# SBUF placement of matmul operands, by their distance modulo 256 bytes, in a hybrid decoder block

## Chip, cores and metric

One Trainium2 chip, one of its cores. The time is device microseconds of one execution of the program; where several executions are shown, the median counts.

## What is computed

One block of a hybrid decoder on `x` of 1 x 256 x 1024 (float32): a normed input feeds three token mixers (retention, a gated short convolution, sparse attention), their outputs are merged by gates, and a gated feed-forward follows.

```python
h = rms_norm(x, attn_norm_w)
z = h @ w_in
y_ret, y_sc, y_nsa = retention(...), sb * causal_dwconv(sc * sx), nsa_attention(...)
merged = g_ret * (y_ret @ w_ret_out) + g_sc * (y_sc @ w_sc_out) + g_nsa * (y_nsa @ w_nsa_out)
x = x + merged @ w_mix_out
u = causal_dwconv(rms_norm(x, ffn_norm_w) @ w_ffn_up)
a, v = split(u); x = x + (silu(a) * v) @ w_ffn_down
return rms_norm(x, final_norm_w)
```

## The kernel before, in words

All weights come from memory as float32 in pieces of 128 x 2048. A piece is an `Item`: `load` brings it in two halves of 128 x 1024 into the ring `raw` (line 123), `split` makes of each half a high part `whi` (ScalarE, line 131) and a remainder `wlo` (VectorE, line 132), both of the type float32r, in a ring of five pairs (line 114, later three more, line 957, and for a while one pair `w_m`, line 319). A product is three matmuls, high by high, high by low, low by high (`mm3`, line 158). `stream` (line 170) walks a list of items, loading two ahead and splitting one ahead; its order and that of `items` set the order of all work, and TensorE takes its instructions in that order.

There are two ways to multiply by a piece. `f_consume` (line 188) makes an output with features on the partitions: the weights are the operand that is loaded into the array (128 columns at a time), the activations `hT`, `xw`, `x2w` or `h2` stream past, 256 columns (all tokens); a piece is 48 matmuls of 256 columns. The pieces kc, vc, ks, kw, nq, scx, sb, rq, rk and up are of this kind. `t_pair` (line 205) and `dn_consume` (line 1078) make an output with tokens on the partitions: 128 tokens of the activations are loaded, and 512 columns of the weights stream. The pieces mg, rv, rg, o_sc, o_nsa, o_ret, mix and dn are of this kind.

**Where the operands lie.** A tile takes its bytes per partition behind the one before it in its pool, pool after pool, in steps of 32 bytes; what counts here is the place modulo 256 bytes, and the distance of a matmul is the place of its loaded operand less that of its streamed one. `whi` and `wlo` (4,096 bytes), `hTh`, `hTl` (8,192), `rstd` and `ones` (1,024 and 512) are multiples of 256, so `whi`, `wlo` and `hT` are at distance 0 of each other. Then comes `x_s` (line 238) of `HD + 2048` columns; with `HD = 32` that is 8,320 bytes, 128 more than a multiple of 256. So `ynsah`, `ynsal` (line 241; `x2w`, line 962, takes their place later) and `yscl` (line 242) lie 128 bytes off, while `ysch`, which takes the place of `x_s`, doesn't. `mT` (line 958) takes the places of `ysch` and `yscl`: one at 0, one at 128. The 64 bytes of `line`, with `warm` and `rs0` of 32 each, bring what follows back to 0: `w_m`, the six `thg` buffers (line 718), `yreth`, `yretl`, `act` and the second ring. `h2` (line 1039) takes the place of `hT`.

The attention scores (`soft_step`, line 529) load `qs` and stream the keys `kdh`, `kdl`, at 128 x 272 and, for the second 128 tokens, 128 x 256 columns. A row of keys is 528 columns for each of four groups, 2,112 bytes or 64 modulo 256, so the distance goes with the group: 160, 96, 32 and 224 bytes for groups 0 to 3 with 272 columns (`qs` lies 160 bytes behind `kd`), and 64 less for those of 256 columns, whose keys start 272 columns (1,088 bytes) on.

| operands of line 156 | columns streamed | matmuls | distance before |
|---|---|---|---|
| `hT`, `h2` by `whi`, `wlo` | 256 | 1,920 | 0 |
| `x2w` by `whi`, `wlo` | 256 | 192 | 128 |
| `xw` (`ynsah`, `ynsal`) by `whi`, `wlo`, `w_m`, kc and vc | 256 | 96 | 128 |
| weights by `hT`, `yret`, `act` (mg, rv, rg, o_ret, dn) | 512 | 840 | 0 |
| weights by `ynsah`, `ynsal` (o_nsa) | 512 | 96 | 128 |
| weights by `ysch` / `yscl` (o_sc) | 512 | 64 / 32 | 0 / 128 |
| weights by `mT` (mix) | 512 | 64 / 32 | 0 / 128 |

Of the kernel before, what the change touches and what calls it, by code (L numbers as in the profile page):

```python
# [11 lines left out]
F32 = mybir.dt.float32  # L12
F32R = mybir.dt.float32r
# [5 lines left out]
S = 256  # L19
D = 1024  # L20
KB = 8
# [15 lines left out]
CM_Z, CM_T, CM_C0, CM_C1, CM_ANY, CM_BLK, CM_SEL = 0, 128, 384, 400, 416, 418, 422  # L37
CM_N = 486

HD = 32  # L40


def _schedule():
# [20 lines left out]
def kernel(  # L64
# [24 lines left out]
    wpool = ctx.enter_context(pool("wpool"))  # L89
# [15 lines left out]
    RAWB, SPB = 4, 5  # L105
    WARM = 8

    def ring(p, nb):
        def get():
            return [p.tile([128, 1024], F32R, tag=n, name=n, bufs=nb) for n in ("whi", "wlo")]  # L110

        return [get] * nb

    splitters, count = ring(wpool, SPB), [0]

    class Item:
        def __init__(self, srcs, consume, pull=0):
            self.srcs, self.consume, self.pull = srcs, consume, pull
            self.raw, self.parts = [], []

        def load(self):
# [4 lines left out]

        def split(self):
            for (ap, n), r in zip(self.srcs, self.raw):
                hi, lo = splitters[count[0] % len(splitters)]()
                count[0] += 1  # L130
                A.copy(hi[:, :n], r[:, :n])  # L131
                V.tensor_sub(lo[:, :n], r[:, :n], f32(hi[:, :n]))  # L132
                self.parts.append((hi, lo))
# [5 lines left out]
    def then(it, f, before=False):  # L139
        old = it.consume  # L140

        def go(parts):
            if before:
                f()
            old(parts)
            if not before:
                f()

        it.consume = go
        return it  # L150

    def piece(name, i, consume, **kw):
        return Item(halves(name, i), consume, **kw)
# [34 lines left out]
    def f_consume(act, evac, kmajor=False):  # L188


        def go(parts):
            ah, al = act() if callable(act) else act
            ps = bank("mm")
            order = [(b, k) for k in range(KB) for b in range(2)] if kmajor else [(b, k) for b in range(2) for k in range(KB)]
            for n, (b, k) in enumerate(order):
                hi, lo = parts[b]
                c = slice(k * 128, (k + 1) * 128)
                o = ps[:, b * 256 : (b + 1) * 256]
                start = n == 0 if kmajor else k == 0
                mm3(o, (hi[:, c], lo[:, c]), (ah[:, k, :], al[:, k, :]), start, k == KB - 1)  # L200
            evac(ps)

        return go
# [25 lines left out]


    yp = mix_es.enter_context(pool("yp"))
    hT = [yp.tile([128, KB, S], F32R, tag=n, name=n) for n in ("hTh", "hTl")]
    M = []
    rstd = yp.tile([128, S], F32, name="rstd")
    ones = yp.tile([128, 128], F32, name="ones")
# [7 lines left out]
    nc.scalar.dma_start(x_s[:, 0 : HD + S], xh)  # L243
    V.memset(ones, 1.0)
    V.memset(mhalf, -0.5)
    yp.tile([128, 16], F32, name="line")
    warm = yp.tile([128, 2], F32, name="warm")
    A.activation(warm, mhalf, AF.Exp)
    pw = bank("aux")
# [47 lines left out]
    def head_h(half):  # L297
        for k in range(4 * half, 4 * half + 4):
            V.scalar_tensor_tensor(xT_s[:, k, :], xT_s[:, k, :], attw(k), rstd, op0=OP.mult, op1=OP.mult)  # L299
            if k % 2 == 1:  # L300
                c = slice(k - 1, k + 1)
                A.copy(hT[0][:, c, :], xT_s[:, c, :])
                V.tensor_sub(hT[1][:, c, :], xT_s[:, c, :], f32(hT[0][:, c, :]))  # L303
# [12 lines left out]
    cp_es = ExitStack()  # L316
    cp = cp_es.enter_context(pool("cp"))

    splitters += [lambda: (lambda z: (z[:, 0, :], z[:, 1, :]))(yp.tile([128, 2, 1024], F32R, tag="m", name="w_m"))]
    blk = {}  # L320

    def cmp_raw_evac(kv):
        def evac(ps):
            p4 = ps.rearrange("p (b t) -> p b t", b=2)
            d = cp.tile([128, 4, S], F32, tag="dd", name="dd", bufs=2)
            dv = d.rearrange("p (b two) t -> p b two t", two=2)
            for par in range(2):
                r = slice(par * 64, par * 64 + 64)
                V.tensor_tensor(dv[0:64, :, par, :], p4[r], rstd[r].unsqueeze(1).to_broadcast([64, 2, S]), op=OP.mult)  # L329
            nc.scalar.dma_start(d[64:128, :, 0 : S - 1], d[0:64, :, 1:S])  # L330
            later(lambda: cmp_blocks(kv, d))

        return evac
# [16 lines left out]
    def key_evac(name):  # L350
        def evac(ps):
            p4 = ps.rearrange("p (b t) -> p b t", b=2)
            for par in range(2):
                r = slice(par * 64, par * 64 + 64)
                o = slice(64 - par * 64, 128 - par * 64)
                kv4 = [k.rearrange("p (b two) t -> p b two t", two=2) for k in kd]
                for t in range(2):
                    c = KCOL[(name, t)]
                    src = p4[r, :, t * 128 : (t + 1) * 128]
                    dst = [k[r, :, par, c : c + 128] for k in kv4]  # L360
                    A.copy(dst[0], src)
                    V.tensor_sub(dst[1], src, f32(dst[0]))  # L362
                c = min(KCOL[(name, t)] for t in range(2))
                for k in kv4:
                    nc.gpsimd.dma_start(k[o, :, par, c : c + 256], k[r, :, par, c : c + 256])

        return evac
# [148 lines left out]
    def q_evac(g):  # L516
        def evac(ps):
            p4 = ps.rearrange("p (b t) -> p b t", b=2)
            qs = at.tile([128, 2, 2, S], F32R, tag="qs", name="qs", bufs=2)
            for par in range(2):  # L520
                r = slice(par * 64, par * 64 + 64)
                o = slice((1 - par) * 64, (1 - par) * 64 + 64)
                A.mul(qs[r, par], p4[r], 0.125)
                V.scalar_tensor_tensor(qs[o, par], p4[r], 0.125, f32(qs[r, par]), op0=OP.mult, op1=OP.subtract)
            qs_t[g] = qs

        return evac
# [149 lines left out]
    def scx_evac(j):  # L677
        def evac(ps):
            sx = sc_tmp.tile([128, S], F32, tag="sx", name="sx", bufs=1)
            A.copy(sx, ps[:, S : 2 * S])  # L680
            V.tensor_mul(sx, ps[:, 0:S], sx)
            u = sc_tmp.tile([128, S], F32, tag="u", name="u", bufs=4)
            conv3(sx, [cvt[:, CV_SC + 8 * i + j : CV_SC + 8 * i + j + 1] for i in range(3)], u)
            sc_prod[j] = u

        return evac

    def sb_evac(i):
        def evac(ps):
            for b in range(2):  # L690
                j = 2 * i + b
                u = sc_prod[j]
                V.tensor_mul(u, ps[:, b * S : (b + 1) * S], u)
                A.copy(ysc[0][:, j, :], u)
                V.tensor_sub(ysc[1][:, j, :], u, f32(ysc[0][:, j, :]))

        return evac
# [1 line left out]
    rsh = at.tile([128, 2], F32, name="rsh")  # L699

    def scx(j, **kw):
        return piece("scx", j, f_consume(hT, scx_evac(j)), **kw)

    def sbp(j, **kw):
        return piece("sb", j, f_consume(hT, sb_evac(j)), **kw)

    def nqp(g, **kw):
        return piece("nq", g, f_consume(hT, q_evac(g)), **kw)

    def head_rest():  # L710
        head_rstd()
# [3 lines left out]

    def mg_evac(n, c):
        def evac(t, ps):
            th = yp.tile([128, 512], F32, tag="thg", name="thg", bufs=6)
            A.activation(th, ps, AF.Tanh, scale=0.5)
            thg[n, c, t] = th  # L720

        return evac
# [37 lines left out]
    def proj(n, **kw):  # L760
# [2 lines left out]
    vv = vv_items()  # L763
    g_sc = gate("o_sc")
    items = vv + [
        then(piece("kc", 0, f_consume(xw, cmp_raw_evac(0))), lambda: head_h(0), before=True),
        then(piece("vc", 0, f_consume(xw, cmp_raw_evac(1))), lambda: head_h(1), before=True),
        piece("ks", 0, f_consume(hT, key_evac("ks"))),
        piece("kw", 0, f_consume(hT, key_evac("kw"))),
        g_sc[0],  # L770
        piece("w1", 0, w1_consume(0, 0)),
        nqp(0),
# [166 lines left out]
                ret_out(us[i - 2])  # L939
            yield  # L940

    items = [piece("r" + n, i, f_consume(hT, rope_evac(n, i))) for n in "qk" for i in range(2)]
    for c in range(2):
        items += t_pair("rv", 2 * c, hT, rv_evac(c))
    items += t_pair("rg", 0, hT, rg_evac(0))
# [90 lines left out]

    def ffn_h():

        h2.extend(yp.tile([128, KB, S], F32R, tag=n, name="h2") for n in ("hTh", "hTl"))
        for c in range(4):  # L1040
            hf = fp.tile([128, 2, S], F32, tag="hf", name="hf", bufs=1)
            ks = slice(2 * c, 2 * c + 2)
            V.tensor_tensor(hf, x2T[:, ks, :], rstd.unsqueeze(1).to_broadcast([128, 2, S]), op=OP.mult)
            A.copy(h2[0][:, ks, :], hf)
            V.tensor_sub(h2[1][:, ks, :], hf, f32(h2[0][:, ks, :]))
# [91 lines left out]

    for j in range(NF):
        act = x2w if j < NX else lambda: h2
        it = piece("up", j, up_early(j) if j < 2 else f_consume(act, up_evac(j)))  # L1140
        if j == NX - 1:
            then(it, ffn_h, before=True)
        items.append(it)
        if j % 2 == 1 and j >= 3:
            items.append(piece("dn", j // 2 - 1, dn_consume(j // 2 - 1)))
# [115 lines left out]
```

## Time and profile before

| | us |
|---|---|
| median of 3 executions | 633.57 (632.41 to 634.73) |
| the profiled execution | 633.64 |
| its span, first to last instruction | 631.9 |
| TensorE busy in it | 611.0 |
| VectorE, ScalarE, GpSimd busy | 477.9, 387.9, 21.2 |

The span has, in order: value pieces, keys and compression (to 62 us), queries, short convolution and attention with gates between (to 282 us), retention inputs and retention (to some 366 us), gates, `o_ret` and `mix` (to 435 us), and the feed-forward (to 623 us). A matmul's record begins when it starts and ends by a model some time after the next has started, so records overlap, and the rate of the engine is read from starts or from the chain, not from durations alone. PEld is the load of a matmul's weights; it runs beside the matmul before.

### The profile page before, as it was taken

What the parts mean: (1) busy time and instruction counts of PE and PEld (TensorE: products, weight loads), DVE (VectorE), ACT (ScalarE), POOL (GpSimd) and SP (SyncE); (2) the same over time, 40 slices, a digit from 0 to 9 for tenths busy, and PEclk for the clock granted to TensorE, in tenths of its full rate; (3) what the DMA queues carried; (4) which work ended last, traced back from release to release, by engine and by line L of the source; (5) the groups of instructions that cost most, each with busy time, mean ns of one, the idle gap of its engine ahead of it and who ended that gap; (6) DMA issues with size and microseconds to landing.
All of it is one profiled execution on the core that took longest, in us unless ns stands there. A gap on an engine that the chain in (4) does not pass through costs nothing.

```text
span 631.9 us, 10611 instructions
## 1 busy us (share of the span) xinstructions
PE 611.0 (97%) x3948; PEld 554.9 (88%) x3948; DVE 477.9 (76%) x935; ACT 387.9 (61%) x752; POOL 21.2 (3%) x32
## 2 busy tenths in 40 slices
PE   8986999999999999999999999999999999999994
PEld 7986989999999888899888888888999999999993
DVE  5897667898988877679657976568798777777754
ACT  6665666788888887644545565446756555554532
POOL 4202000000000000000000000000000000000001
PEclk8999999999999999999999999999999999999997
DMA  7759876444354344465664477575347655566401
GB/s 247 239 160 271 243 248 206 135 166 135 104 163 135 108 153 140 134 213 169 203 198 160 133 242 260 192 269 172 108 152 264 213 183 175 183 198 199 136 1 66
DMA packets 32995, 111.80 MB, mean 177 GB/s; under 512 B 3632, under 2 KB 5552, under 8 KB 32816
## 3 DMA queue, kind: packets, MB, share of 16 engines
q1 hardware_dynamic: 30240, 106.00, 51.8%
q10 hardware_dynamic: 1552, 4.08, 2.0%
q0 software_dynamic: 1152, 1.05, 1.1%
q8 instruction: 31, 0.51, 0.3%
q14 instruction: 20, 0.16, 0.1%
HBM read 108.50 MB, written 1.05 MB: 173 GB/s over the span
## 4 chain that ended last, share of the span: by engine, by line
PE 82%; DVE 6%; ACT 5%; DMA 4%; POOL 1%; issue 1%; SPq 0%; POOLq 0%; ACTq 0%
PE ps_mm L156 61%; PE ps_aux L156 18%; DMA raw<-in_wp_dram 3%; DVE wlo L132 2%; ACT whi L131 2%; PE ps_aux L589 1%; DMA xT_s<-in_xT_dram 1%; ACT P L566 1%; POOL sq L272 0%; PE ps_aux L618 0%; DVE hTl L303 0%; DVE dd L329 0%; DVE xT_s L299 0%; ACT low L632 0%; DVE bb L347 0%
## 5 line engine op out<-in xcount | busy, mean ns | idle before, releaser
L132 DVE TENSOR_TENSOR wlo<-raw,whi 128x1024 fp32r<-128x1024 f32 (+1 forms) x197 | 237.7, 1210 | 90.7 <-ACT whi L131 88.7
L131 ACT CAST whi<-raw 128x1024 fp32r<-128x1024 f32 (+1 forms) x197 | 203.2, 1035 | 140.0 <-PE ps_mm L156 98.0
L156 PE MATMUL ps_mm<-hTh,whi 128*128 128x256 f32 x352 | 101.0, 287 | 6.1 <-DVE kdl L362 5.1
L156 PE MATMUL ps_mm<-h,whi 128*128 128x256 f32 x576 | 104.0, 283 | 0.0
L156 PE MATMUL ps_mm<-hTl,whi 128*128 128x256 f32 x352 | 100.4, 285 | 0.6 <-DVE hTl L303 0.6
L156 PE MATMUL ps_mm<-hTh,wlo 128*128 128x256 f32 x352 | 100.5, 285 | 0.3 <-DVE wlo L132 0.2
L156 PEld LDWEIGHTS ps_mm<-h,whi 128*128 128x128 f32 x576 | 90.4, 192 | 0.7
L156 PE MATMUL ps_mm<-h,wlo 128*128 128x256 f32 x288 | 81.5, 283 | 0.0
L156 PEld LDWEIGHTS ps_mm<-hTh,whi 128*128 128x128 f32 x352 | 68.1, 193 | 6.7 <-issue 5.2
L156 PEld LDWEIGHTS ps_mm<-hTl,whi 128*128 128x128 f32 x352 | 68.1, 193 | 1.3 <-DVE hTl L303 1.0
L156 PEld LDWEIGHTS ps_mm<-hTh,wlo 128*128 128x128 f32 x352 | 68.1, 194 | 0.7 <-DVE wlo L132 0.7
L156 PE MATMUL ps_mm<-whi,hTh 128*128 128x512 f32 x152 | 59.7, 393 | 0.0
L156 PE MATMUL ps_mm<-wlo,hTh 128*128 128x512 f32 x152 | 59.3, 390 | 0.0
L156 PE MATMUL ps_mm<-whi,hTl 128*128 128x512 f32 x152 | 59.3, 390 | 0.0
L156 PEld LDWEIGHTS ps_mm<-h,wlo 128*128 128x128 f32 x288 | 55.3, 192 | 0.0
L566 ACT ACTIVATE P<-P,st 128x16 f32<-128x16 f32 (+2 forms) x96 | 37.9, 397 | 0.7 <-DVE st L561 0.7
L156 PE MATMUL ps_aux<-wlo,acth 128*128 128x512 f32 x88 | 34.4, 390 | 0.0
L156 PE MATMUL ps_aux<-whi,acth 128*128 128x512 f32 x88 | 34.4, 390 | 0.0
L156 PE MATMUL ps_aux<-whi,actl 128*128 128x512 f32 x88 | 34.3, 389 | 0.0
L156 PEld LDWEIGHTS ps_mm<-whi,hTl 128*128 128x128 f32 x152 | 28.5, 188 | 6.1
L156 PEld LDWEIGHTS ps_mm<-whi,hTh 128*128 128x128 f32 x152 | 28.6, 188 | 5.6
L156 PEld LDWEIGHTS ps_mm<-wlo,hTh 128*128 128x128 f32 x152 | 28.6, 188 | 5.6
(250 smaller groups left out, 1140.9 us busy)
## 6 DMA issues: line engine op xcount, KB each, us to landing
raw<-in_wp_dram SPq DMA_DIRECT2D x194, 512.0 KB, 4.4
raw<-in_wv_dram SPq DMA_DIRECT2D x8, 280.0 KB, 4.8
x2b<-in_xt_dram ACTq DMA_DIRECT2D x1, 1024.0 KB, 7.2
xT_s<-in_xT_dram SPq DMA_DIRECT2D x3, 256.0 KB, 6.9
rct<-in_rc_dram ACTq DMA_DIRECT2D x1, 768.0 KB, 6.1
kdh<-kdh POOLq DMA_DIRECT2D x4, 128.0 KB, 6.1
kdl<-kdl POOLq DMA_DIRECT2D x4, 128.0 KB, 6.9
finb<-in_fin_dram ACTq DMA_DIRECT2D x1, 512.0 KB, 3.5
```

Of the source, the lines that this page charges most:

```text
L131: A.copy(hi[:, :n], r[:, :n])
L132: V.tensor_sub(lo[:, :n], r[:, :n], f32(hi[:, :n]))
L156: return T.matmul(o, l, r, start=start, stop=stop, skip_group_check=True)
L566: A.activation(pp, pp, AF.Exp, bias=st[:, r : r + 1], scale=-1.0, accum_out=sm[:, r : r + 1])
L589: T.transpose(pt[:, dst : dst + 128], u["P"][(t, pr)][:, c : c + 128], ident)
```

## The change

It alters places in memory only. The list of instructions of each engine, their order and what each waits for stay as they are, but for the first transfer, which is 320 columns wide in place of 288.

- `HD` is 64: `x_s` takes 8,448 bytes, a multiple of 256, and `line` grows from 64 to 192 bytes. `ynsah`, `ynsal`, `yscl`, `x2w` and the second `mT` come to the place 0.
- The buffers of the first ring are 64 columns (256 bytes) wider. An item has a `side`: its weights start 16 columns (64 bytes) into the buffer if it is of the 256-column kind (nq, scx, sb, kc, vc, ks, kw, rq, rk, and the first four up pieces), and at 0 otherwise. The second ring and `w_m` have no such room; there weights start at 0.
- `hT` is 256 bytes wider and starts at 0; `h2` starts 48 columns (192 bytes) into the same room, so that weights at 0 are 64 bytes behind it modulo 256.
- `thg` has four buffers in place of six.

| operands of line 156 | columns | matmuls | distance before | after |
|---|---|---|---|---|
| `hT`, `h2` by weights | 256 | 1,920 | 0 | 64 |
| `x2w` by weights | 256 | 192 | 128 | 64 (120), 0 (72) |
| kc and vc | 256 | 96 | 128 | 64 (72), 0 (24) |
| o_nsa; the 128 halves of o_sc and mix | 512 | 160 | 128 | 0 |
| other weights, streamed | 512 | 968 | 0 | 0 |
| attention scores | 272, 256 | 96 | by group | the same |

```diff
-HD = 32
+HD = 64
...
-    def ring(p, nb):
-        def get():
-            return [p.tile([128, 1024], F32R, tag=n, name=n, bufs=nb) for n in ("whi", "wlo")]
+    SIDE = 16
+
+    def ring(p, nb, room=0):
+        def get(o):
+            o = min(o, room)
+            return [p.tile([128, 1024 + room], F32R, tag=n, name=n, bufs=nb)[:, o : o + 1024] for n in ("whi", "wlo")]
...
-    splitters, count = ring(wpool, SPB), [0]
+    splitters, count = ring(wpool, SPB, 4 * SIDE), [0]
...
-        def __init__(self, srcs, consume, pull=0):
-            self.srcs, self.consume, self.pull = srcs, consume, pull
+        def __init__(self, srcs, consume, pull=0, side=0):
+            self.srcs, self.consume, self.pull, self.side = srcs, consume, pull, side
...
-                hi, lo = splitters[count[0] % len(splitters)]()
+                hi, lo = splitters[count[0] % len(splitters)](self.side)
...
-    hT = [yp.tile([128, KB, S], F32R, tag=n, name=n) for n in ("hTh", "hTl")]
+    def shifted(tag, name, o):
+        t = yp.tile([128, KB * S + 4 * SIDE], F32R, tag=tag, name=name)
+        return t[:, o : o + KB * S].rearrange("p (k t) -> p k t", k=KB)
+
+    hT = [shifted(n, n, 0) for n in ("hTh", "hTl")]
...
-    yp.tile([128, 16], F32, name="line")
+    yp.tile([128, 48], F32, name="line")
...
-        return piece("scx", j, f_consume(hT, scx_evac(j)), **kw)
+        return piece("scx", j, f_consume(hT, scx_evac(j)), side=SIDE, **kw)
...
-            th = yp.tile([128, 512], F32, tag="thg", name="thg", bufs=6)
+            th = yp.tile([128, 512], F32, tag="thg", name="thg", bufs=4)
...
-        h2.extend(yp.tile([128, KB, S], F32R, tag=n, name="h2") for n in ("hTh", "hTl"))
+        h2.extend(shifted(n, "h2", 3 * SIDE) for n in ("hTh", "hTl"))
...
-        it = piece("up", j, up_early(j) if j < 2 else f_consume(act, up_evac(j)))
+        it = piece("up", j, up_early(j) if j < 2 else f_consume(act, up_evac(j)), side=SIDE if j < NX else 0)
```

## Rows read from the trace of the kernel before

**Rows 1.** The page: span, busy time of the engines, granted clock by slice.
```profile
span 631.9 us, 10611 instructions
...
PE 611.0 (97%) x3948; PEld 554.9 (88%) x3948; DVE 477.9 (76%) x935; ACT 387.9 (61%) x752; POOL 21.2 (3%) x32
...
PEclk8999999999999999999999999999999999999997
```
**Rows 2.** Stretches: length, busy us of each engine (instructions), granted clock, DMA share, GB/s.
```profile
core 0: us, PE busy (x) PEld busy (x) DVE busy (x) ACT busy (x) POOL busy (x), PEclk, DMA share, GB/s
0.00:62.50 62.50, 51.75 (x353) 48.13 (x353) 47.94 (x76) 39.04 (x62) 14.95 (x23) 0.97 0.79 228
62.50:282.00 219.50, 217.89 (x1506) 200.46 (x1507) 174.06 (x475) 165.49 (x419) 0.58 (x1) 0.99 0.51 163
282.00:330.00 48.00, 48.00 (x253) 41.43 (x253) 34.57 (x41) 23.32 (x27) 0.00 (x0) 1.00 0.60 192
330.00:411.00 81.00, 81.00 (x397) 68.00 (x396) 60.09 (x95) 43.36 (x57) 2.79 (x4) 1.00 0.59 197
411.00:465.00 54.00, 53.92 (x342) 48.33 (x341) 42.62 (x70) 33.59 (x53) 1.10 (x2) 1.00 0.50 169
465.00:623.00 158.00, 158.00 (x1104) 148.49 (x1103) 115.15 (x175) 80.50 (x130) 0.00 (x0) 1.00 0.51 167
```
**Rows 3.** Waits of TensorE, 62.5 us to the end: us in total, times, longest.
```profile
PE ps_mm L156 <- DVE kdl L362: 5.1, 1, 5.1
PE ps_aux L618 <- ACT pc L574: 0.8, 2, 0.5
PE ps_aux L428 <- DVE cq_lo L419: 0.2, 1, 0.2
PE ps_aux L156 <- ACT ph L592: 0.2, 1, 0.2
```
**Rows 4.** Timeline of TensorE: start us, us, what, [idle before <-releaser].
```profile
62.47 0.55 PE L156 MATMUL ps_mm<-hTh,whi 128*128 128x256 f32 x1 [5.06 <-DVE kdl L362]
```
**Rows 5.** The chain, 465 to 476.5 us: start us, us, what, pieces.
```profile
465.18 11.39 PE ps_mm L156 x95
```
**Rows 6.** Tile `h` (`h2`), 466 to 476 us: duration ns min/median/max, first and last start.
```profile
L156 PE MATMUL ps_mm<-h,whi x58: 283/283/283, 465.7 to 475.9; 128*128 128x256 f32 x58
L156 PEld LDWEIGHTS ps_mm<-h,whi x56: 192/192/192, 466.0 to 475.8; 128*128 128x128 f32 x56
```
**Rows 7.** The chain, 448.2 to 459.4 us.
```profile
448.18 11.27 PE ps_mm L156 x95
```
**Rows 8.** Tile `x2w`, 448.2 to 459.2 us: duration ns min/median/max.
```profile
L156 PEld LDWEIGHTS ps_mm<-x2w,whi x64: 187/188/189, 448.0 to 459.2; 128*128 128x128 f32 x64
L156 PE MATMUL ps_mm<-x2w,whi x63: 279/281/285, 448.1 to 459.2; 128*128 128x256 f32 x63
```
**Rows 9.** The chain, 378 to 388 us (`o_ret`).
```profile
377.87 10.20 PE ps_mm L156 x45
```
**Rows 10.** The chain, 354 to 358.8 us (`o_nsa`).
```profile
353.87 5.11 PE ps_mm L156 x22
```
**Rows 11.** Groups, 378 to 388 us: busy us, mean ns of one | idle before.
```profile
L156 PE MATMUL ps_mm<-wlo,yreth 128*128 128x512 f32 x16 | 6.2, 389 | 0.0
```
**Rows 12.** Groups by form, 177 to 215.5 us: scores of group 2.
```profile
L156 PE MATMUL ps_aux<-kdl,qs 128*128 128x272 f32 x8 | 2.3, 289 | 0.0
L156 PE MATMUL ps_aux<-kdh,qs 128*128 128x272 f32 x8 | 2.3, 286 | 0.0
```
**Rows 13.** Groups by form, 137.5 to 165 us: scores of group 1.
```profile
L156 PE MATMUL ps_aux<-kdh,qs 128*128 128x272 f32 x5 | 1.4, 288 | 0.0
L156 PE MATMUL ps_aux<-kdh,qs 128*128 128x256 f32 x2 | 0.6, 280 | 0.0
```
**Rows 14.** Groups by form, 282 to 450 us: transposes, which come in fours.
```profile
L744 PE MATMUL ps_mm<-ident,hnb 128*128 128x128 f32 x16 | 2.4, 272 | 0.0
```
**Rows 15.** Groups by form, 411.5 to 422 us (`mix`).
```profile
L156 PE MATMUL ps_aux<-whi,mT 128*128 128x512 f32 x28 | 9.0, 396 | 0.0
L156 PE MATMUL ps_aux<-wlo,mT 128*128 128x512 f32 x15 | 5.9, 396 | 0.0
```

More of the change, by code (lines that the diff above doesn't have):

```diff
@@ L317 @@
     cp = cp_es.enter_context(pool("cp"))
-    splitters += [lambda: (lambda z: (z[:, 0, :], z[:, 1, :]))(yp.tile([128, 2, 1024], F32R, tag="m", name="w_m"))]
+    splitters += [lambda o: (lambda z: (z[:, 0, :], z[:, 1, :]))(yp.tile([128, 2, 1024], F32R, tag="m", name="w_m"))]
     blk = {}
@@ L701, in scx @@
     def scx(j, **kw):
-        return piece("scx", j, f_consume(hT, scx_evac(j)), **kw)
+        return piece("scx", j, f_consume(hT, scx_evac(j)), side=SIDE, **kw)
     def sbp(j, **kw):
-        return piece("sb", j, f_consume(hT, sb_evac(j)), **kw)
+        return piece("sb", j, f_consume(hT, sb_evac(j)), side=SIDE, **kw)
     def nqp(g, **kw):
-        return piece("nq", g, f_consume(hT, q_evac(g)), **kw)
+        return piece("nq", g, f_consume(hT, q_evac(g)), side=SIDE, **kw)
     def head_rest():
@@ L765 @@
     items = vv + [
[L766 to L769, printed above, removed]
+        then(piece("kc", 0, f_consume(xw, cmp_raw_evac(0)), side=SIDE), lambda: head_h(0), before=True),
+        then(piece("vc", 0, f_consume(xw, cmp_raw_evac(1)), side=SIDE), lambda: head_h(1), before=True),
+        piece("ks", 0, f_consume(hT, key_evac("ks")), side=SIDE),
+        piece("kw", 0, f_consume(hT, key_evac("kw")), side=SIDE),
         g_sc[0],
@@ L940, in retention @@
             yield
-    items = [piece("r" + n, i, f_consume(hT, rope_evac(n, i))) for n in "qk" for i in range(2)]
+    items = [piece("r" + n, i, f_consume(hT, rope_evac(n, i)), side=SIDE) for n in "qk" for i in range(2)]
     for c in range(2):
```

## The prediction

> **What bounds the kernel now.** I read the page first, then the stretches, the waits of TensorE, and last the spacing of single matmuls. The page shows TensorE busy for 611.0 of 631.9 us, with the granted clock in the top tenth in nearly all slices [rows 1]. Busy is not the same as full speed, so the table of stretches matters more: from 62.5 to 623 us TensorE is busy 558.8 of 560.5 us, with VectorE at 72 to 79% and ScalarE at 49 to 75% [rows 2]. The waits of TensorE named after that point amount to 0.8, 0.2 and 0.2 us, beside one of 5.1 us for the key copies of line 362, which ends at 62.47 us [rows 3, 4]. So behind 62.5 us nobody is waited for, and the time is the number of matmuls times the spacing between their starts. Ahead of it the DMA engines are 79% busy [rows 2] and TensorE waits; what the change saves there I count as nothing.
>
> The spacing is the disputed quantity. In two FFN-up pieces on `h2` 95 matmuls of 256 columns take 11.39 us on the chain, 119.9 ns each [rows 5], and every record is alike: 283 ns, and 192 ns for each weight load [rows 6]. The granted clock is 1.00 there [rows 2], the level of 2.4 GHz, at which 256 columns are 106.7 ns of streaming; 13 ns are lost each time. In two pieces on `x2w`, which differ in that the activations lie 128 bytes further on, the chain has 95 in 11.27 us, 118.6 ns each [rows 7]; the records vary from 279 to 285 ns and a weight load takes 187 to 189 ns [rows 8]. With 512 columns it is the other way round: 45 matmuls on `yret` (distance 0) take 10.20 us, 226.7 ns each [rows 9], against 22 on `ynsa` (128) in 5.11 us, 232.3 ns each [rows 10]. Records and starts agree: a record is about 163 ns longer than the spacing (283 and 119.9; 389 and 226.7 [rows 11]), which turns durations into spacings below. Same shape, same engine, another distance, another spacing: that is the evidence that the distance matters at all.
>
> **The change part by part.** No instruction is added, removed, moved or given another wait; one transfer at the start grows by 32 columns. So every term is a number of matmuls times a difference in spacing.
>
> *256 columns, distance 0 to 64.* Twenty pieces on `hT` (4 nq, 8 scx, 4 sb, 4 rq and rk) and 18 FFN-up pieces on `h2`, 48 matmuls each: 1,824 that lie behind 62.5 us. No pair of this shape at 64 bytes is in the trace, so I bound it. The nearest distances are in the attention scores, where the group index moves the keys by 64 bytes against the queries. At 32 bytes the 272-column records last 286 and 289 ns [rows 12], at 96 bytes 288 [rows 13]; sixteen columns are 6.7 ns at 2.4 GHz, so that is a spacing of 287.5 - 163 - 6.7 = 117.8 ns and of 118.3 ns for 256 columns. The 256-column records in the second window are themselves at 32 bytes (their keys start 272 columns on) and last 280 ns, a spacing of 117 [rows 13]. But those come in pairs, between other matmuls. At distance 0 a whole piece repeats one spacing and one weight load of 192 ns, while at 128 bytes a load takes 187 to 189: a pair that leaves distance 0 loses a repeated delay of about 4 ns, 120 to 116. Between that 116 and the neighbours' 117 I take 116.5 ns: 1,824 x 3.4 ns = 6.2 us. Bound from below: transposes, with 128 columns and so half the streaming, still last 272 ns [rows 14], a spacing of 109, the pace of the weight loads alone; 1,824 x 10.9 ns = 19.9 us. Bound from above: 119.9, nothing gained, and for harm the last rival.
>
> A page's price, by itself: the Trainium skill, "TensorE: Matmul & The Clock Gate", section "Back-to-back issue gap", gives an isolated matmul at the higher clock N/2.4 + 2.5 ns, 109.2 ns for 256 columns. By that, if 64 bytes took away all of the loss, the gain would be an estimated 19.5 us; no stretch read here runs that fast, nor do the 512-column ones (226.7 measured, 215.8 by the page).
>
> *256 columns, distance 128 to 64 or 0.* The four FFN-up pieces on `x2w`, 192 matmuls: five of eight halves get 64 bytes, three, in the second ring, 0. 120 x (118.6 - 116.5) - 72 x (119.9 - 118.6) ns = 0.2 us. The pieces before 62.5 us: nothing, behind transfers.
>
> *512 columns, distance 128 to 0.* Here the weights stream and the activations are loaded. `o_sc`, `o_nsa` and `mix` have 96 matmuls each. `o_nsa` pays 232.3 against 226.7 [rows 10, 9]. In `mix` the records are 396 ns against the 389 of `yret` [rows 15, 11]; there only one of the two tensors is off, and a pair loses where the distance changes as well. `o_sc` is placed like `mix`, but attention work lies between its matmuls. I take 5 ns for 288: 1.4 us, with 0.7 and 2.0 as ends.
>
> *The `thg` ring from six buffers to four, wider tiles, the longer first transfer.* Nothing: at most four gates are alive at once, and the waits of the program are the same; 16 KB more are lost in the first stretch.
>
> *What comes next.* A piece of 48 matmuls would take 5.59 us in place of 5.76. From 465 to 623 us VectorE has 115 of 158 us, ScalarE 80, the DMA engines 51% [rows 2]; a stretch 3 to 6% shorter leaves all under 80%, and nobody takes TensorE's place. In the attention (62.5 to 282 us) VectorE has 174 of 219.5 us and the softmax chains now and then just miss their turn [rows 3]; of a gain of some 3 us there, 0.2 may come back as waits.
>
> Sum: 6.2 + 0.2 + 1.4 - 0.2 = 7.6 us. The profiled execution took 633.64 us, 1.7 more than its span and within 0.1 us of the median of 633.57, so the sum serves for both: **626.0 us**, 1.2% less.
>
> **The rivals.**
>
> *A deeper gain.* At 64 bytes the two reads could fall in step so that a good spacing repeats, as the bad one does at distance 0. For it: rows 6 show that a constant distance can hold one state for whole pieces. Against it: no mean read here is under 117. Halfway from 117 to the pace of the weight loads is 113: 1,824 x 6.9 ns + 120 x 5.6 ns + 1.4 us = 14.7 us, 618.9 us; I count 615 to 622 as this case. Chance 0.22.
>
> *The distance does nothing.* As a mechanism in these rows: the 13 ns are a fixed cost of each matmul, rows 9 and 10 differ because retention runs beside `o_nsa`, and the time stays 633.6 us. The Trainium skill, "SBUF — State Buffer", section "Who interferes with whom", would have it so: it gives TensorE two independent read ports, for the streamed operand and for the weights, and says that it never waits on anyone. The trace doesn't agree: a weight load is 192 ns in rows 6 and 188 in rows 8, the same form in the same stage. Chance 0.05. A milder form, in which 64 bytes is as good as 0 and only the 512-column term holds, gives 633.6 - 1.4 = 632.2 us. For it: the neighbours are worth only 1.6 to 2.9 ns. Chance 0.10.
>
> *A worse collision, slower than before.* The weight read could meet the activation read more often at 64 bytes than at 0, in each of the 1,824 matmuls. Price: the harm that 128 bytes does to 512 columns, 5.6 ns [rows 9, 10]: 10.2 us, so 633.6 + 10.2 - 1.4 = 642.4 us. It decides from a spacing of 120.7 ns on, where the harm eats the 1.4 us. For it: a distance can be worse than 0, as rows 10 show. Against it: the 256-column records at 32 and 128 bytes are 280 and 281, none over 283 on average. Chance 0.08.
>
> **How the numbers follow.** The forecast, a spacing of 115 to 119 and so 622 to 631 us, has 0.55, the deeper gain 0.22, the milder form 0.10, no effect at all 0.05, slower 0.08. Faster by over 0.3% (1.9 us, what a measurement here can tell from no change) is under 631.7 us: 0.55 + 0.22 and a quarter of the milder form, where the 512-column term reaches 2.0 us: 0.79. Within 0.3%: the rest of the milder form and no effect, 0.13. Slower: 0.08. The range leaves out the slower case, no effect at all, and the part of the deeper gain under 618 us (0.07): 618 to 632.6 us.
>
> **What would show it.** Right: two pieces on `h2` with 95 spacings in about 11.07 us, records near 280 ns and weight loads of 187 to 189 in place of a uniform 283 and 192; `o_nsa` and `mix` at 389 in place of 394 to 396; TensorE's waits unchanged. Wrong: the `h2` records still read 283 (no effect), 276 or less (deeper), over 284 (harm), or they fall and the span doesn't, in which case a wait has come up, most likely in the attention.

## The result and the profile after

The change takes 626.05 us (median of 4 executions, 624.39 to 626.24) against 633.67 us (632.41 to 634.73) measured beside it for the kernel before: a ratio of 0.9873, 95% interval 0.9853 to 0.9894. The forecast was 626.0.

The page of the changed kernel: span, busy times, granted clock by slice.

```profile
span 624.3 us, 10611 instructions
...
PE 603.4 (97%) x3948; PEld 548.2 (88%) x3948; DVE 477.6 (76%) x935; ACT 387.1 (62%) x752; POOL 21.2 (3%) x32
...
PEclk9999999999999999999999999999999999999998
```

The span fell by 7.6 us, TensorE's busy time by the same 7.6 (611.0 to 603.4); VectorE's moved by 0.3 [rows 1]. The count of instructions is the same.

The same stages as in [rows 2], cut at the same matmuls:

```profile
core 0: us, PE busy (x) PEld busy (x) DVE busy (x) ACT busy (x) POOL busy (x), PEclk, DMA share, GB/s
0.00:60.94 60.94, 51.14 (x353) 47.79 (x353) 48.00 (x76) 38.22 (x62) 14.96 (x23) 1.00 0.81 231
60.94:277.85 216.91, 214.36 (x1506) 196.85 (x1507) 173.62 (x474) 165.97 (x419) 0.58 (x1) 0.99 0.52 166
...
459.59:615.52 155.93, 155.93 (x1105) 146.63 (x1103) 115.17 (x175) 80.63 (x130) 0.03 (x1) 1.00 0.51 169
```

Read the first column of each row against that of [rows 2]: 1.6 us less in the first stage, 2.6 in queries and attention (219.5 to 216.9), 2.1 in the feed-forward (158.0 to 155.9); the three stages between, left out here, end 1.3 us sooner together (183.0 to 181.7). Behind the second stage TensorE is busy in all but 0.2 of 337.7 us. The waits of TensorE from the key copies to the end, beside [rows 3]:

```profile
PE ps_mm L161 <- DVE kdl L371: 5.2, 1, 5.2
PE ps_aux L627 <- ACT pc L583: 1.2, 2, 0.7
PE ps_aux L437 <- DVE cq_lo L428: 0.5, 2, 0.3
PE ps_aux L161 <- ACT ph L601: 0.2, 1, 0.2
PE ps_mm L161 <- ACT x2T L1018: 0.2, 1, 0.2
```

Those behind the key copies rise from 1.2 to 2.1 us: a faster TensorE seems to arrive a little sooner at the softmax (`pc`, `ph`) and at the compressed queries (`cq_lo`).

**Spacings.** The spacing is the time from the start of one matmul to the start of the next. On `h2`, the chain and the tile answer to [rows 5, 6]:

```profile
459.75 11.31 PE ps_mm L161 x96
```
```profile
L161 PE MATMUL ps_mm<-h,whi x56: 281/281/281, 460.3 to 469.9; 128*128 128x256 f32 x56
L161 PEld LDWEIGHTS ps_mm<-h,whi x54: 187/188/188, 460.5 to 469.8; 128*128 128x128 f32 x54
L161 PEld LDWEIGHTS ps_mm<-h,wlo x28: 192/192/192, 460.4 to 470.0; 128*128 128x128 f32 x28
```

96 matmuls in 11.31 us are 117.8 ns each, and records and loads repeat to the nanosecond; but only two of three weight loads lost the delay, the one of `wlo` still takes 192 ns. All 18 up pieces on `h2` are like this. On `hT`, at the same distance of 64 bytes, another picture (sb and the retention pieces at 271 to 287 us):

```profile
270.88 16.09 PE ps_mm L161 x142
```
```profile
L161 PE MATMUL ps_mm<-hTh,wlo x43: 276/276/276, 271.4 to 285.7; 128*128 128x256 f32 x43
...
L161 PEld LDWEIGHTS ps_mm<-hTh,whi x43: 187/188/188, 271.4 to 285.7; 128*128 128x128 f32 x43
L161 PEld LDWEIGHTS ps_mm<-hTh,wlo x43: 187/188/188, 271.6 to 285.9; 128*128 128x128 f32 x43
```

142 in 16.09 us are 113.3 ns, records of 276 and every load 187 or 188. The record of a load is a sign of the spacing and not its price: one load of three that is 4 ns longer would be 1.3 ns a matmul, and the spacings of 117.8 and 113.3 differ by 4.5. The starts show the `hT` pieces to be a mixture of the two: of 960 from the key copies on 562 are followed after 113 or 114 ns and 360 after 115 to 125. Long rows hold one value, and a change comes where a piece begins or where attention work stands between. With 512 columns, `o_nsa` (the chain), `o_ret` (groups by form at 378 to 388 us) and `mix` (at 406 to 416 us) answer to [rows 10, 11, 15]:

```profile
341.01 5.47 PE ps_mm L161 x24
```
```profile
L161 PE MATMUL ps_mm<-wlo,yreth 128*128 128x512 f32 x8 | 3.1, 389 | 0.0
...
L161 PE MATMUL ps_aux<-whi,mT 128*128 128x512 f32 x27 | 8.7, 393 | 0.0
L161 PE MATMUL ps_aux<-wlo,mT 128*128 128x512 f32 x14 | 5.5, 390 | 0.0
```

`o_nsa` goes at 227.9 ns in place of 232.3, `o_ret` keeps its records of 389 and its 226.7 ns (the mean of its 96 starts in either trace), the `mix` records drop from 396 to 390 and 393.

**Where the 7.6 us lie.** The instruction list is the same, so I took the starts of the same matmul in both traces. The 413th starts at 72.4 us before and at 70.8 after; the last one starts 7.5 us earlier. Between them, summed from start to next start:

| | matmuls | before, us | after, us | gain |
|---|---|---|---|---|
| ahead of the 413th | 412 | 72.43 | 70.79 | 1.6 |
| `hT` | 912 | 112.88 | 109.67 | 3.2 (of which stalls -0.8) |
| `h2` | 864 | 103.61 | 101.76 | 1.85 |
| `x2w` | 192 | 23.06 | 22.96 | 0.1 |
| `o_nsa`, `mix`, `o_sc` | 288 | 68.25 | 67.38 | 0.9 (0.43, 0.31, 0.13) |
| all other | 1,279 | 242.83 | 242.96 | -0.1 |

A stall here is a next start that comes over 140 ns later; `hT` has 22 in both traces, and ten of them stand just ahead of attention work.

Behind the 413th matmul 5.9 us are gained, and nearly all of them are spacing. The 1.6 us ahead of it are another matter. The granted clock of the first stage is 0.97 before [rows 2] and 1.00 after, and from 55 to 73 us it differs from run to run, whatever the places. Of the ten kernels here with `hT` at 64 bytes, one trace each, the five with a mean of 0.91 there start the 413th matmul at 70.4 to 71.7 us, mean 71.1; the five with 0.81 start it at 71.2 to 73.0, mean 71.9. So how much of the 1.6 us the places gave is not shown.

### The profile page after: what moved, and what is told of

Read it like the earlier page. It is cut to its first block, busy times and chain, and to the rows that moved or that the text cites. A ratio compares the mean times of both kernels' runs of the same rounds, so it can differ in the third digit from the quotient of the medians.

```text
span 624.3 us, 10611 instructions
## 1 busy us (share of the span) xinstructions
PE 603.4 (97%) x3948; PEld 548.2 (88%) x3948; DVE 477.6 (76%) x935; ACT 387.1 (62%) x752; POOL 21.2 (3%) x32
## 3 DMA queue, kind: packets, MB, share of 16 engines
q0 software_dynamic: 1152, 1.05, 1.2%
HBM read 108.51 MB, written 1.05 MB: 175 GB/s over the span
## 4 chain that ended last, share of the span: by engine, by line
PE 76%; DVE 7%; ACT 7%; DMA 6%; issue 2%; POOL 1%; SPq 0%; POOLq 0%; ACTq 0%; DVEq 0%
PE ps_mm L161 56%; PE ps_aux L161 17%; DMA raw<-in_wp_dram 5%; DVE wlo L137 3%; ACT whi L136 2%; PE ps_aux L598 1%; ACT P L575 1%; DMA xT_s<-in_xT_dram 1%; DVE qs L533 0%; POOL sq L281 0%; PE ps_aux L627 0%; DVE hTl L312 0%; DVE dd L338 0%; DVE xT_s L308 0%; ACT low L641 0%
## 5 line engine op out<-in xcount | busy, mean ns | idle before, releaser
L161 PE MATMUL ps_mm<-hTh,whi 128*128 128x256 f32 x352 | 99.4, 282 | 6.2 <-DVE kdl L371 5.2
L161 PE MATMUL ps_mm<-h,whi 128*128 128x256 f32 x576 | 102.2, 281 | 0.0
L161 PE MATMUL ps_mm<-hTh,wlo 128*128 128x256 f32 x352 | 99.0, 281 | 0.5 <-DVE wlo L137 0.5
L161 PE MATMUL ps_mm<-hTl,whi 128*128 128x256 f32 x352 | 98.8, 281 | 0.6 <-DVE hTl L312 0.6
L161 PEld LDWEIGHTS ps_mm<-h,whi 128*128 128x128 f32 x576 | 88.5, 188 | 0.7
```

The costliest lines, as they stand in the source:

```text
L161: return T.matmul(o, l, r, start=start, stop=stop, skip_group_check=True)
```

## The experiments

Theory at the outset: the time is the number of matmuls times a spacing that the distance of a matmul's two operands sets. Rivals: the gain comes from one of the two kinds of matmul only; it is not the own pair but the next weights against the present stream that counts; and, once two states had been seen at one distance, that the way into a piece chooses between them or that chance does. In the diffs a place in bytes is four times the number of columns. The runs on the FFN from the third on, but the cut at distance 0, share this edit, which gives the second ring room and puts `h2` at 0, so that each distance is set by the weights:

```diff
-    splitters += ring(wpool2, 3)
+    splitters += ring(wpool2, 3, 4 * SIDE)
...
-        h2.extend(shifted(n, "h2", 3 * SIDE) for n in ("hTh", "hTl"))
+        h2.extend(shifted(n, "h2", 0) for n in ("hTh", "hTl"))
```

### The 512-column part alone

All weights and `h2` at 0; only the wider `HD` and `line` remain, so `x2w` and the kc and vc pieces go from 128 to 0 as well.

```diff
-        return piece("scx", j, f_consume(hT, scx_evac(j)), side=SIDE, **kw)
+        return piece("scx", j, f_consume(hT, scx_evac(j)), side=0, **kw)
...
-        h2.extend(shifted(n, "h2", 3 * SIDE) for n in ("hTh", "hTl"))
+        h2.extend(shifted(n, "h2", 0) for n in ("hTh", "hTl"))
...
```

(The same `side=0` stands in the other pieces.)

> HD, line and the wider buffers as in the change, but every weight tile and h2 start at 0: 512-column pairs go from 128 to 0, all 256-column pairs on hT and h2 stay at 0, x2w goes from 128 to 0. Theory (spacing depends on the distance, terms add): 288 matmuls x about 4.5 ns less, 192 on x2w x 1.3 ns more, so 1.0 us under the kernel before, ratio 0.9984, with o_nsa and mix spacings at 227 in place of 232 and h2 locked at 120.0 ns. Rival (the distance does nothing, the whole gain has another source): the ratio is 1.000 or already 0.987.

Measured: 633.35 us against 633.98 (medians of 12 and 17 executions), ratio 0.9984 (0.9971 to 0.9997). The chain, `o_nsa` and then an up pair on `h2`:

```profile
345.99 5.47 PE ps_mm L161 x24
...
464.92 11.51 PE ps_mm L161 x96
```

`o_nsa` at 227.9 ns as in the change, `h2` at 119.9 as before: the two parts can be taken apart, and this one is worth 1.0 us by the ratio (0.2 to 1.8 by its interval) and 0.6 by the medians. The four `thg` buffers, which were not tried alone, are in this run and so in this gain.

### The 256-column part alone

```diff
-HD = 64
+HD = 32
...
-    yp.tile([128, 48], F32, name="line")
+    yp.tile([128, 16], F32, name="line")
...
-        it = piece("up", j, up_early(j) if j < 2 else f_consume(act, up_evac(j)), side=SIDE if j < NX else 0)
+        it = piece("up", j, up_early(j) if j < 2 else f_consume(act, up_evac(j)), side=0)
```

(The kc and vc pieces have no `side` here, so they lie as before the change.)

> The weights 64 bytes behind hT and h2 as in the change, but HD = 32 and line = 64 bytes again, so that all 512-column pairs, kc, vc and x2w lie as before. Theory: 960 matmuls on hT at some 115 ns and 864 on h2 at 117.8 in place of 119.9, 6.5 us under the kernel before, ratio 0.9898; with only_512 the two gains add up to that of the change within 0.5 us. Rival (the two parts interact, for instance through the state in which a 512-column piece hands over): the sum of the two gains misses that of the change by over 1 us.

Measured: 628.37 us against 633.98, ratio 0.9911 (0.9888 to 0.9934), 5.6 us. `o_nsa` and an up pair:

```profile
342.60 5.58 PE ps_mm L161 x24
...
461.92 11.31 PE ps_mm L161 x96
```

`o_nsa` is back at 232.5 ns, `h2` at 117.8; the starts on `hT` have a mean of 115.0 (stalls left out). The parts add up to -1.05% where the whole has -1.27%, which the intervals allow. That the distance does nothing falls here: nothing but places (and the width of the first transfer) differs between these two kernels, and each moves the spacing of its own kind.

### Distances one by one

Up pairs at nine distances, with dn at 0; then dn pieces (512 columns) at eleven, with all up pairs at 64; then up pairs again, with dn at 192.

```diff
+    UPD = [64, 64, 32, 32, 96, 96, 0, 0, 128, 128, 48, 48, 160, 160, 80, 80, 192, 192]
+    DND = [0, 0, 0, 0, 0, 0, 0, 0, 0, 0, 0]
...
-        it = piece("up", j, up_early(j) if j < 2 else f_consume(act, up_evac(j)), side=SIDE if j < NX else 0)
+        it = piece("up", j, up_early(j) if j < 2 else f_consume(act, up_evac(j)), side=SIDE if j < NX else UPD[j - NX] // 4)
...
-            items.append(piece("dn", j // 2 - 1, dn_consume(j // 2 - 1)))
+            items.append(piece("dn", j // 2 - 1, dn_consume(j // 2 - 1), side=DND[j // 2 - 1] // 4))
...
```

In the second run `UPD` is 64 throughout and `DND` is 0, 192, 224, 128, 160, 64, 96, 32, 240, 16, 208; as weights stream there, the distance is 256 less that.

> FFN-up pieces 4 to 21, two of a kind in order, at the distances 64, 32, 96, 0, 128, 48, 160, 80, 192 bytes (weights shifted, h2 not); dn pieces all at 0. Theory (one spacing for a distance, whatever else moves): 64 gives 117.8 again, 0 gives 120.0, 128 gives 118.6, 32 and 96 give 117 to 118. Rival (two locked spacings are possible at a distance, 113.3 and 117.8 at 64, and what went before chooses): 64 may give 113.3 here, and neighbours of 64 show 113.3 as well or a third locked value. Rival (distance does nothing): all 120.

> FFN-down pieces 0 to 10, 24 matmuls of 512 columns each, at the distances 0, 64, 32, 128, 96, 192, 160, 224, 16, 240, 48 bytes (loaded activations less streamed weights); all up pieces at 64. Theory that 0 is the best for 512 columns: 226.7 ns at 0, 229 to 234 at every other. Rival (0 is only better than 128): some distance gives 217 to 222 ns, as 64 gave 113 in place of 120 with 256 columns. The up pieces behind dn pieces at other distances show whether the way in chooses between 113.3 and 117.8: with theory 1 all stay at 117.8, with the rival some fall to 113.3.

> The up pieces at 32, 96, 0, 128, 48, 80, 192, 224, 64, two of each, all dn pieces at 192 in place of 0. Theory (a second, better state exists at 64 alone): 64 gives 113.3, the others what they gave in the first scan, 32: 118.3, 96: 117.4, 0: 120.0, 128: 118.6 or 120.1, 48: 118.3, 80: 118.6, 192: 117.8. Rival (every distance has a better state that the way in at 0 missed): some of the others come under 115.

Measured, mean spacing in ns from the starts (one execution each; 628.03, 627.17 and 626.04 us):

| distance | 0 | 16 | 32 | 48 | 64 | 80 | 96 | 128 | 160 | 192 | 224 | 240 |
|---|---|---|---|---|---|---|---|---|---|---|---|---|
| 256 columns, dn at 0 | 119.9 | | 118.3 | 118.3 | 117.8 | 118.6 | 117.4 | 120.1 | 119.9 | 117.8 | | |
| 256 columns, dn at 192 | 120.0 | | 118.3 | 118.4 | 113.6 | 118.8 | 118.6 | 118.7 | | 117.8 | 117.8 | |
| 512 columns | 227.7 | 233.2 | 233.7 | 230.0 | 233.5 | | 234.6 | 232.3 | 233.8 | 229.0 | 233.4 | 231.8 |

(The 118.3 at 32 bytes with dn at 192 is the second piece of the pair; its first piece holds a wait.)

For 512 columns 0 is the best place tried, with 192 next; so the change's choice of 0 there holds. A dn piece at 192 is not fixed to one spacing either: in the third run most take 229 ns and two, behind up pieces at 80 and 192, take 233.4. For 256 columns every distance but 64 gives 117.4 to 120.1, and 64 gives either 117.8 or 113.3 (113.6 with the first starts of the pair). Each other distance was entered once or twice, so a faster state there is not excluded. The way in matters elsewhere too, by less: 96 bytes came at 117.4 and at 118.6, 128 at 120.1 and at 118.7. The chain of the second run shows the same 96 matmuls at 64 bytes behind dn pieces (x24) at 0, 64, 32 and 128:

```profile
461.49 11.31 PE ps_mm L161 x96
472.79 5.60 PE ps_aux L161 x24
478.39 10.89 PE ps_mm L161 x96
489.29 5.61 PE ps_aux L161 x24
494.89 11.31 PE ps_mm L161 x96
...
511.78 10.89 PE ps_mm L161 x96
```

11.31 or 10.89 us and nothing between: two states at one distance, and something in what goes ahead seems to decide which. The faster one, 113.3 ns, is called the good state from here on. A state holds for both pieces of a pair; of the nine pairs five are in the faster one.

### The next weights, or the own ones

The weights of a matmul are read while the one before it streams (from 465 to 623 us loads are busy for 148.49 us beside a TensorE that is busy throughout [rows 2]), so the distance that counts could be that of the next weights to the present stream. Here the next weights are always 64 bytes behind the present stream, while the own distances are 64, 0 and 128.

```diff
-        it = piece("up", j, up_early(j) if j < 2 else f_consume(act, up_evac(j)), side=SIDE if j < NX else 0)
+        it = piece("up", j, up_early(j) if j < 2 else f_consume(act, up_evac(j)), side=SIDE if j < NX else (SIDE, 2 * SIDE))
...
-        h2.extend(shifted(n, "h2", 0) for n in ("hTh", "hTl"))
+        h2.extend(shifted(n, "h2", SIDE * (n == "hTl")) for n in ("hTh", "hTl"))
```

(`whi` at 64, `wlo` at 128; `h2` at 0 and 64. `ring` takes the two offsets.)

> In the FFN-up pieces on h2 the three matmuls of a triple get different distances of their own: 64 (high by high), 0 (high by low) and 128 (low by high), placed so that the weights loaded next stand 64 bytes behind the activations that stream meanwhile, all three times. Theory 'next' (the load of the next weights collides with the streaming of the present activations): one uniform spacing of 117.8 or 113.3. Theory 'own' (what counts is a matmul's own pair): the triple mixes 64, 0 and 128, 118 to 120 ns with an uneven pattern, and no 113.3.

Measured: 627.11 us in one execution. The chain and the tile `h`, 494 to 504 us:

```profile
493.59 11.37 PE ps_mm L161 x96
```
```profile
L161 PE MATMUL ps_mm<-h,whi x58: 279/281/286, 493.8 to 503.9; 128*128 128x256 f32 x58
L161 PEld LDWEIGHTS ps_mm<-h,whi x57: 187/188/193, 494.0 to 504.0; 128*128 128x128 f32 x57
```

118.4 ns and uneven: the one uniform spacing that the theory of the next weights asks for did not come, so a next distance of 64 alone does not make a piece behave like those with all distances at 64. That 113.3 is missing says little by itself, since behind dn pieces at 0 the uncut pairs at 64 did not reach it either.

### Another neighbour: all FFN weights 64 bytes in

If the dn pieces at 192 let the up pieces into the good state, they should in every pair.

```diff
-        it = piece("up", j, up_early(j) if j < 2 else f_consume(act, up_evac(j)), side=SIDE if j < NX else 0)
+        it = piece("up", j, up_early(j) if j < 2 else f_consume(act, up_evac(j)), side=SIDE)
...
-            items.append(piece("dn", j // 2 - 1, dn_consume(j // 2 - 1)))
+            items.append(piece("dn", j // 2 - 1, dn_consume(j // 2 - 1), side=SIDE))
```

> All weights of the feed-forward 64 bytes into their buffers, h2 at 0: up pieces at 64 as in the change (and all of the x2w ones), dn pieces at 192. Theory (two locked spacings at 64, the way in chooses): behind a dn piece at 192 the scan fell to 113.3, so 864 matmuls on h2 gain 4.4 ns less some transients, 3.6 us, x2w gains 0.2 and the dn pieces lose about 2 ns x 264 = 0.5: 3.2 us under the change, about 622.9, ratio to the kernel before 0.982. Rival (the state in the scan came from whatever stood before in that scan, not from 192): the up pieces stay at 117.8 or mix, and the time is the change's or 0.5 us over it.

Measured: 628.06 us against 633.51, ratio 0.9886 (0.9847 to 0.9924); six executions with 627.81, 622.01, 628.88, 628.31, 628.83 and 623.28. A miss. In the profiled one every pair stayed where it was:

```profile
477.56 11.31 PE ps_mm L161 x96
...
494.38 11.31 PE ps_mm L161 x96
```

So the neighbour's place alone does not decide; all nine pairs repeat what the first began with. Two executions of six are 5 to 6 us shorter, about what all FFN pieces at 113.3 would give (1,056 matmuls x 4.5 ns = 4.8 us). That these were in the other state throughout is inferred: only one execution has a trace.

### The phase at the way in

What differs between two entries with the same neighbours can be the moment. To shift it, the first matmul of a pair is cut into two by columns, at another column in each of the nine pairs; all weights of up at 64, dn at 0.

```diff
-    def f_consume(act, evac, kmajor=False):
+    def f_consume(act, evac, kmajor=False, cut=0):
...
+                if cut and n == 0:
+                    for a in (slice(0, cut), slice(cut, S)):
+                        mm(o[:, a], hi[:, c], ah[:, k, a], a.start == 0, False)
+                    mm(o, hi[:, c], al[:, k, :], False, False)
+                    mm(o, lo[:, c], ah[:, k, :], False, False)
+                    continue
...
+    CUT = [0, 128, 64, 192, 32, 224, 16, 96, 160]
...
-        it = piece("up", j, up_early(j) if j < 2 else f_consume(act, up_evac(j)), side=SIDE if j < NX else 0)
+        it = piece("up", j, up_early(j) if j < 2 else f_consume(act, up_evac(j), cut=CUT[(j - NX) // 2] if j >= NX and j % 2 == 0 else 0), side=SIDE)
```

> Everything at the places of the change (up at 64, dn at 0), but the first matmul behind each dn piece is cut in two by columns: 0 (not cut), 128, 64, 192, 32, 224, 16, 96, 160 columns first, for the nine pairs of up pieces. Each cut adds one matmul, some 110 ns. Theory (the phase at the way in chooses between two states that last): some pairs hold 113.3 through both pieces and others 117.8, the uncut one 117.8. Rival (the place or the distance of the dn weights chooses): all stay at 117.8.

Measured: 624.44 us in one execution. The chain, with the pairs of the cuts at 0 (none), 128, 64, 192, 32, 224 and 16:

```profile
459.77 11.31 PE ps_mm L161 x96
...
476.54 11.02 PE ps_mm L161 x97
...
493.02 11.01 PE ps_mm L161 x97
...
509.50 11.01 PE ps_mm L161 x97
...
525.97 11.02 PE ps_mm L161 x97
...
542.45 11.03 PE ps_mm L161 x97
...
558.94 11.41 PE ps_mm L161 x97
```

The uncut pair at 459.77 and the one cut at 16 (558.94) stay at 117.8; the other five, and the two that follow (cuts at 96 and 160), fall to 113.3 within some eight starts and hold it through the second piece, which has no cut. So seven of eight cuts reach the good state. A cut costs some 0.1 us (11.02 against the 10.89 of an uncut pair in that state), and a pair gains 0.3. A cut at 128, 64 or 192 columns leaves the places of both halves modulo 256 as they were, and all three changed the state; so with the same neighbours and the same places, the moment of the way in chooses. (The cut at 16 is the only one whose second half lies 64 bytes further on; whether it failed for that or for its moment is not separated.)

### The cut where distance is 0

The same cuts in the kernel before, nothing else changed.

> The kernel before, all places as they were (h2 at distance 0), with the first matmul behind the dn pieces cut at 0, 128, 64, 192, 32, 224, 16, 96 and 160 columns. Theory (the faster state exists at 64 bytes alone): every up piece locks at 120.0 whatever the cut, each pair costs 11.51 us or up to 0.05 more, and the time is that of the kernel before within 0.3%. Rival (a cut is worth the same whatever the distance, because it shifts the phase against something else): most pairs fall by 0.3 us or more, to 11.2, and the time to about 631.2 us.

Measured: 635.33 us in one execution (the kernel before: 629.65 to 635.71 beside it). An uncut pair and a cut one:

```profile
466.04 11.51 PE ps_mm L156 x96
...
483.02 11.61 PE ps_mm L156 x97
```

Within some dozen starts every pair is back at 120.0; the cuts only cost, 0.1 us each. So a cut is worth nothing by itself: at 64 bytes the same eight cuts reached 113.3 seven times, at 0 never.

### Using it

One cut at 128 columns at the head of each pair and of the third `x2w` piece, in several executions; and the same with sixteen more at the heads of the nq, scx and sb pieces.

```diff
-        it = piece("up", j, up_early(j) if j < 2 else f_consume(act, up_evac(j)), side=SIDE if j < NX else 0)
+        it = piece("up", j, up_early(j) if j < 2 else f_consume(act, up_evac(j), cut=128 if j % 2 == 0 else 0), side=SIDE)
```

> All FFN-up weights 64 bytes behind their activations, and the first matmul of the first up piece behind every dn piece (and of the third x2w piece) cut into two of 128 columns. Theory (two locked states at 64 bytes, and the phase of the way in chooses): the 864 matmuls on h2 go at 113.3 ns in place of 117.8; a pair costs 11.01 us in place of 11.31 with its cut, nine pairs 2.7 us; with the x2w pieces 0.2 to 0.7 us more. 626.0 - 2.7 - 0.4 = about 622.9 us, ratio 0.983 to the kernel before. Rival (the state is set by something that varies from run to run, and the cut of the first look met it by luck): some pairs stay at 117.8 and the time lies between 623 and 626, ratio 0.983 to 0.988, with single runs of either kind.

> As the kernel with cuts in the FFN, and the same cut at the head of the sixteen nq, scx and sb pieces on hT. Theory: seven of eight pieces land at 113.3 behind a cut, so the mean over the hT pieces falls from the 115.1 of the change to about 113.9: 768 x 1.2 ns = 0.9 us less than with the FFN cuts alone, about 622.0 us, ratio 0.9815. Rival: behind attention work the way in varies anyway, a cut spoils as many good pieces as it mends, the mean stays near 115, and the time is that of the FFN cuts or up to 0.5 us over it.

Measured: with the cuts in the FFN 623.99 us against 633.6, ratio 0.9856 (0.9828 to 0.9883), six executions from 623.34 to 625.07. It is the fastest kernel here by its median, 2 us under the change, though the interval overlaps the change's. The forecast was 622.9. Of the 1.1 us that are missing 0.4 are the first pair; in the profiled execution (623.72 us) another 0.6 lie ahead of the 413th matmul, which starts at 71.4 in place of 70.8 us.

```profile
459.29 11.46 PE ps_mm L161 x97
...
476.21 11.02 PE ps_mm L161 x97
```

Eight pairs take 11.0 us, the first 11.46. The timeline in it, of VectorE (first row) and of TensorE:

```profile
460.68 0.68 DVE L1060 TENSOR_TENSOR h<-hf,h 128x512 fp32r<-128x512 f32 x1
...
460.96 0.39 PE L161 MATMUL ps_mm<-h,whi 128*128 128x256 f32 x2
461.18 0.28 PE L161 MATMUL ps_mm<-h,wlo 128*128 128x256 f32 x1
461.30 0.50 PE L161 MATMUL ps_mm<-h,whi 128*128 128x256 f32 x2
461.63 0.28 PE L161 MATMUL ps_mm<-h,wlo 128*128 128x256 f32 x1
```

Up to 461.4 it ran at 113.3; then one start came 222 ns behind the one before it, twice the usual, and everything behind it in the pair goes at 117.8. TensorE's waits name nothing there, but the place does: it is the first matmul that needs the low part of the last quarter of `h2`, which VectorE (line 1060) finishes at 461.35; the load for that matmul starts at 461.41, 0.22 us behind the load before it in place of 0.11. In the run on the next weights the first pair is held at the same matmul, for long enough to be named:

```profile
461.16 0.68 DVE L1054 TENSOR_TENSOR h<-hf,h 128x512 fp32r<-128x512 f32 x1
```
```profile
461.90 0.19 PEld L161 LDWEIGHTS ps_mm<-h,whi 128*128 128x128 f32 x1 [0.21 <-DVE h L1054]
```

There too the load starts 0.05 us behind VectorE's end. So the first pair, which starts 0.5 us earlier than in the change and runs faster, catches up with the making of `h2`, and one start 109 ns late was enough to change the state.

With the further cuts on `hT`: 627.48 us, ratio 0.9901 (0.9875 to 0.9927), a miss. The share of `hT` starts at 113 or 114 ns does rise, 661 of 944 uncut ones against 605 of 960 with the FFN cuts alone; that is some 66 x 4.5 ns = 0.3 us. But from the 413th matmul on the summed starts of `hT`, its halves with it, rise by 2.2 us. The two halves of a cut take 168 to 257 ns from their start to the next matmul (457 once) where a whole matmul takes 113, which is 1.7 us over the sixteen; the waits of TensorE named between the key copies and 292 us rise by 0.7. The cuts spend more than they mend.

## Why the prediction was right, and where only by its sum

- *The bound.* TensorE bounds the kernel behind the key copies, and the time is count times spacing: right. The span and TensorE's busy time fell by the same 7.6 us, 5.9 of it behind the 413th matmul.
- *256 columns on `hT` and `h2`, 116.5 ns.* Right as a mean: (960 x 115.2 + 864 x 117.8) / 1,824 = 116.4, stalls left out. Wrong as a picture, and so the mean is in part luck: no long row of the changed kernel ran at 116.5. The step "a pair that leaves distance 0 loses a repeated delay of about 4 ns, 120 to 116" took one spacing for one distance. The runs showed two at 64 bytes, 117.8 (one of three loads still delayed, 192 ns) and 113.3 (none). `h2` gained 1.85 us where 3.4 ns each would be 2.9; `hT` made up for most of it, 4.0 us without its stalls where 3.1 would be due. The records of `h2` at 281 answer to "near 280", the loads of `wlo` at 192 don't answer to "187 to 189", and on `hT` the good rows read 276, the sign that the prediction had set for the deeper gain.
- *512 columns.* 1.4 forecast, 0.9 from the starts, 1.0 by the run of that part alone, inside the ends of 0.7 and 2.0. `o_nsa` was sized right (0.43 us on 96); `o_sc` was not: 0.13 us, its halves hardly move.
- *Before 62.5 us, "I count as nothing".* In the two traces this term is 1.6 us, the start of the 413th matmul. Over the ten traces with `hT` at 64 bytes it starts at 70.4 to 73.0 us, mean 71.5, against 72.4, 72.9 and 73.3 in the three with `hT` at 0: some 1.4 us, with a scatter of nearly twice that, and with the granted clock of the stage varying beside it. Whether the places earned it stays open.
- *Waits given back, 0.2 us.* Mis-sized: 0.9 us, on the softmax and the compressed queries, so the sign "TensorE's waits unchanged" was not met. The 1.6 us ahead that were not counted, against 0.7 more of waits, 0.5 less of the 512-column term and 0.35 less of the 256-column one, are why the sum still came to 7.6. That the total came so close is luck: the waits are four times their size, and the largest miss, the 1.6 us, stood in the sum as nothing.
- *The rivals.* The deeper gain, 0.22, is the half that was real: 113 ns is the measured spacing of the good state, held by 59% of the `hT` starts and by no `h2` piece. "The distance does nothing" is refuted by the two runs of one part each, and its milder form, with the 512-column term alone, by the 5.6 us of the other part. The Trainium skill, "SBUF — State Buffer", section "Who interferes with whom", gives TensorE two independent read ports and says that it never waits on anyone. These runs do not agree: the same matmul takes 120.0 ns at distance 0 and 117.8 or 113.3 at 64 bytes, and between the two distances only places differ. The worse collision did not come for 256 columns; for 512 it exists, and at 64 bytes (233.5 against 227.7).
- *The price of 109.2 ns.* The Trainium skill, "TensorE: Matmul & The Clock Gate", section "Back-to-back issue gap", gives N/2.4 + 2.5 ns for an isolated matmul, 109.2 for 256 columns. No piece here reached that; the fastest hold 113.3.

## What to carry to other kernels

Where one engine is at 97% and repeats one instruction some two thousand times, read the spacing of starts to the nanosecond and compare pieces that differ only in where their operands lie; 4 ns here are 1% of the kernel. The best place tried depends on the shape: activations and weights 64 bytes apart for 256 columns, equal places modulo 256 for 512. Before a mean spacing is used as a price, look whether it is one state or a mixture of two. And before a gain in a stretch that waits is put down to a change, compare the granted clock there.

## What was not expected of the hardware

- At a distance of 64 bytes a row of 256-column matmuls locks into one of two spacings, 113.3 or 117.8 ns, and can hold it over 142 matmuls; the moment of the way in chooses (seven of eight cuts changed it), and one start that came 109 ns late ended it.
- The sign seems to count: 64 bytes reached 113.3, 192 bytes (the same distance the other way round) stayed at 117.8 in both runs; that is one pair in each.
- For 512 columns every distance tried but 0, 192 and 48 costs 4 to 7 ns a matmul (231.8 to 234.6 against 227.7). A period of 256 bytes fits: the buffers of the widened first ring take 4,352 bytes each, an odd multiple of 256, and all 18 up pieces on `h2` still take 117.8 ns in the change. What in the chip makes 256 bytes the period was not tried.
